# The residual stream of a decoder's FFN is added in the last chunk of hidden pairs instead of the second

## The chip, the cores and the metric

The program runs on 1 core of one Trainium2 chip. The metric is device time in microseconds (us) of one execution. The kernel before takes 2130.71 us, the median of 3 runs (2129.2 to 2131.78).

## What is computed

A trunk of two pre-norm residual layers over a stream of 1024 positions by 1024 features in float32. Layer 0 has a mixer of short convolution and mLSTM, layer 1 a spatial-gating MLP; each layer ends with a SwiGLU FFN, and a final norm follows. The change is in the FFN, which both layers call:

```python
def swiglu(xn, w_in, w_out):
    h = xn @ w_in
    g, up = h[..., :D_FF], h[..., D_FF:]
    return (jax.nn.silu(g) * up) @ w_out

x = x + swiglu(rmsnorm(x, norm_ffn[layer]), ffn_w_in[layer], ffn_w_out[layer])
```

D_FF is 2816, which is 22 slices of 128 hidden features.

## The kernel before

The stream lies transposed, features on the 128 partitions: tile `x[d][c]` holds feature rows `d` (0 to 7) and the position half `c` (0 or 1), 128 x 512 float32, 256 KB. Every product is three matmuls (`mm3`, lines 115 to 117) of a high and a low part.

**The FFN** (`swiglu`, line 390) first makes the hidden slices and stores them, as sums and differences, in DRAM (`hd` for 9 pairs of slices, `td` for the last 4 slices). It then multiplies them by `w_out` with Winograd's scheme of seven block products in place of eight (`STEPS`, line 351; step `s` runs from 0 to 6). The nine pairs are cut into four chunks, `PAIRS = (2, 2, 2, 3)`. A **unit** is one chunk `ch` and one pair of feature rows `dp` (rows 2 dp and 2 dp + 1); there are 16 of them, chunk by chunk and `dp` 0 to 3 in each. A unit of chunks 0 to 2 has 7 x 2 x 3 = 42 matmuls, one of chunk 3 has 7 x 3 x 3 = 63. Chunk 3 is followed by a **tail** (`part`, line 592), which adds the last four slices directly, column half 0 for all eight `d`, then column half 1.

For each unit, SP loads two pieces of weights (`Halves.load`, line 313: tiles `st`, 256 KB each, 384 KB in chunk 3), one unit or two ahead through four buffers; ACT and DVE cut them into high and low parts and their sums (lines 323, 324, 334 to 337). The hidden blocks of the next chunk come in during the current one by `bring` (line 524): tiles `f0h` of 256 KB, 28 for chunks 1 and 2, 42 for chunk 3, 16 for the tail, most of them in the later units of a chunk (`spread` and `ending`, lines 547 and 548). They go on SP's queue, between the weights.

**The results of a unit** go through `sink` (line 498). In chunk 0 they open the tiles `x[d][c]` (`keep`, line 486). In later chunks, steps 0, 1 and 6 add into `x[d][0]` on DVE (line 484), while for `x[d][1]` a difference is first formed in a tile `e` (lines 491 and 494) and then added into `x[d][1]` by a DMA that accumulates, which POOL issues:

```python
def gather(dst, src):
    nc.gpsimd.dma_start(dst, src, accum_op=ALU.add)
```

The stream from before the FFN, `x_in`, is in DRAM. It is added by the same kind of DMA, at the end of a unit: four tiles (two `d`, two `c`), 16 in each layer. Line 510 says in which chunk:

```python
if s == 6 and ch == 1:
    for d in rows:
        for c in range(2):
            gather(x[d][c][:, :HALF], x_in[d * P : (d + 1) * P, c * HALF : (c + 1) * HALF])
```

Everything else that reads `x` comes in the tail (line 601: `x[d][c]` plus the tail's product, on DVE), which then feeds the norm that follows and, in layer 0, a store of `x` to DRAM by POOL (line 254).

A scheduler orders the instructions of each engine beforehand; on the chip each engine's list runs in order, and a DMA waits on the engine that issues it until its semaphores allow it. In the rows below, `f0x<-x_dram` is a transfer of `x_in`, `f0x<-f0e` one of the tiles `e`, both of layer 0; `f1x` and `f1e` are layer 1's.

Of the kernel before, what the change touches and what calls it, by code (L numbers as in the profile page):

```python
# [26 lines left out]
PAIRS = (2, 2, 2, 3)  # L27
# [16 lines left out]
def trunk(ctx, tc, x_t, vecs, b_gate, b_s, ws_t, we, we_v, we_g, we_o, wo_u, wo_v, wo_o, wf_in, wf_out, out_t):  # L44
# [12 lines left out]
    def slot(name, dt=F32):  # L57
        return slots.tile([P, SLOT], dt, tag="s", name=name)
# [328 lines left out]
    def gather(dst, src):  # L387
        nc.gpsimd.dma_start(dst, src, accum_op=ALU.add)  # L388

    def swiglu(layer, normed, todo, spans, after):  # L390
# [87 lines left out]
        def onto(dp, ch):  # L478
            opening = ch == 0
            rows, hold = (2 * dp, 2 * dp + 1), {}  # L480

            def add(d, c, t):
                to = x[d][c][:, :HALF]
                nc.vector.tensor_tensor(to, t, to, op=ALU.add)

            def keep(d, c, ps):
                t = slot(f"{name}x{d}{c}" if opening else f"{name}e{d}{c}")
                if opening:
                    x[d][c] = t
                hold[d, c] = t[:, :HALF]  # L490
                nc.scalar.copy(hold[d, c], ps)

            def less(d, c, p, q):
                nc.vector.tensor_tensor(hold[d, c], p, q, op=ALU.subtract)  # L494
                if not opening:
                    gather(x[d][c][:, :HALF], hold[d, c])

            def sink(s, ps):
                d0, d1 = rows
                if s in (0, 6) and opening:  # L500
                    keep(d0 if s == 0 else d1, 0, ps)
                elif s in (0, 1, 6):
                    add(d1 if s == 6 else d0, 0, ps)
                elif s in (2, 3):
                    keep(d0 if s == 2 else d1, 1, ps)
                elif s == 4:
                    less(d1, 1, hold[d1, 1], ps)
                else:
                    less(d0, 1, ps, hold[d0, 1])
                if s == 6 and ch == 1:  # L510
                    for d in rows:
                        for c in range(2):
                            gather(x[d][c][:, :HALF], x_in[d * P : (d + 1) * P, c * HALF : (c + 1) * HALF])

            return sink
# [626 lines left out]
```

## Time and profile before

| what | value |
|---|---|
| median of the runs | 2130.71 us |
| the profiled execution | 2129.71 us, span 2128.0 us |
| TensorE (PE) busy | 2084.4 us, 98% of the span; mean granted clock 0.992 |
| DVE, ACT, POOL busy | 65%, 39%, 13% of the span |
| DMA | 327.89 MB, mean 154 GB/s; mean busy share of a slice from 0.1 to 0.9 or more |
| of that, on POOL's queue | 116.46 MB |
| chain that ended last | PE 88%, DMA 7%, issue 2%, DVE 2%, ACT 1% |
| transfers of `x_in`, each layer | 16 of 256 KB, 8.1 us (layer 0) and 7.9 us (layer 1) from issue to landing |

How to read it: PE is busy nearly all the time, so the span shortens where PE waits or where its matmuls run slowly. The stretch of the four chunks and the tail is read window by window; in layer 0 chunk 0 ends at 943 us, chunk 2 at 1041, chunk 3 at 1102, in layer 1 at 1914, 2011 and 2068. A DMA share is the mean busy share of the core's 16 DMA engines; it can pass 1 a little.

### The profile page before, as it was taken

How to read it: one execution, taken by the hardware profiler on the slowest of the kernel's cores; microseconds unless marked ns; L12 is line 12 of the kernel's file. 1: busy time of each engine (PE TensorE's matmuls, PEld its weight loads, DVE VectorE, ACT ScalarE, POOL GpSimd, SP SyncE). 2: the span in 40 equal slices, each digit the busy share in tenths (PEclk: the TensorE clock that was granted, in tenths of full speed). 3: DMA queues.
4: the chain of work that ended last, by engine and by line, in shares of the span. 5: the costliest groups of instructions: out<-in, count | busy, mean ns of one | idle time of the engine just before them, and what ended most of it. 6: DMA issues, size and time to landing. Idle time of an engine off the chain costs nothing.

```text
span 2128.0 us, 25497 instructions
## 1 busy us (share of the span) xinstructions
PE 2084.4 (98%) x9294; PEld 1685.9 (79%) x9294; DVE 1377.6 (65%) x2176; ACT 825.0 (39%) x1277; POOL 278.0 (13%) x453
## 2 busy tenths in 40 slices
PE   9999999999999999998999999999999999998998
PEld 7878888888888878875688888888888888876777
DVE  6236665568787777655556666666878777655566
ACT  5111122345444444332235743444444444432234
POOL 0000000003221121103111000002212112103110
PEclk9999999999999999999999999999999999999999
DMA  5121111536453344579974221445534334479962
GB/s 170 59 76 60 45 50 50 198 128 154 155 186 129 138 169 149 199 243 270 304 219 139 89 70 40 168 158 109 198 127 180 129 139 168 142 277 278 335 185 80
DMA packets 131934, 327.89 MB, mean 154 GB/s; under 512 B 17072, under 2 KB 19152, under 8 KB 131808
## 3 DMA queue, kind: packets, MB, share of 16 engines
q1 hardware_dynamic: 88912, 209.77, 28.7%
q0 software_dynamic: 42752, 116.46, 18.8%
q8 instruction: 73, 1.20, 0.2%
q14 instruction: 53, 0.43, 0.1%
q10 hardware_dynamic: 144, 0.03, 0.0%
HBM read 213.98 MB, written 91.24 MB: 143 GB/s over the span
## 4 chain that ended last, share of the span: by engine, by line
PE 88%; DMA 7%; issue 2%; DVE 2%; ACT 1%; POOL 0%; SPq 0%; DVEq 0%; ACTq 0%; POOLq 0%
PE Af1i L115 4%; PE Af1i L116 3%; PE Af1i L117 3%; PE Af0i L115 3%; PE Af0i L116 3%; PE Af0i L117 3%; DMA st_f1o<-wf_out 2%; DMA st_f0o<-wf_out 2%; PE Bf1i L115 2%; PE Bf1i L117 2%; PE Bf1i L116 2%; DMA f1h<-hd 2%; PE Bf0i L116 2%; PE Bf0i L115 2%; PE Bf0i L117 2%
## 5 line engine op out<-in xcount | busy, mean ns | idle before, releaser
L254 POOL DMA_DIRECT2D x_dram<-xe x16 | 8.7, 541 | 452.7 <-DVE xe L268 447.7
L254 POOL DMA_DIRECT2D x_dram<-xo x16 | 8.7, 541 | 276.7 <-DVE xo L268 271.7
L109 ACT CAST hi_eo<-st_eo 128x1024 fp32r<-128x1024 f32 x20 | 21.0, 1049 | 48.9 <-PE ep L116 30.6
L453 DVE TENSOR_TENSOR f1q<-f1q,Af1i 128x512 f32<-128x512 f32 x20 | 13.7, 687 | 36.9 <-PE Af1i L117 36.9
L453 DVE TENSOR_TENSOR f0q<-f0q,Af0i 128x512 f32<-128x512 f32 x20 | 13.7, 687 | 35.6 <-PE Af0i L117 35.6
L323 ACT CAST hix_f0i<-st_f0i 128x1024 fp32r<-128x1024 f32 x20 | 21.1, 1053 | 39.1 <-PE Af0i L116 25.0
L323 ACT CAST hix_f1i<-st_f1i 128x1024 fp32r<-128x1024 f32 x20 | 21.1, 1053 | 38.9 <-PE Af1i L116 25.1
L388 POOL DMA_DIRECT2D f0x<-f0e x24 | 22.5, 1031 | 90.8 <-DVE f0e L494 88.8
L323 ACT CAST hiy_f1i<-st_f1i 128x1024 fp32r<-128x1024 f32 x20 | 21.1, 1054 | 31.2 <-PE Bf1i L116 30.7
L388 POOL DMA_DIRECT2D f1x<-f1e x24 | 21.8, 917 | 87.2 <-DVE f1e L494 81.4
L323 ACT CAST hiy_f0i<-st_f0i 128x1024 fp32r<-128x1024 f32 x20 | 21.1, 1055 | 31.1 <-PE Bf0i L116 30.5
L443 DVE TENSOR_TENSOR f1b<-Cf1i,f1b 128x512 f32<-128x512 f32 x20 | 13.8, 688 | 26.6 <-issue 17.9
L443 DVE TENSOR_TENSOR f0b<-Cf0i,f0b 128x512 f32<-128x512 f32 x20 | 13.7, 687 | 26.6 <-issue 17.9
L116 PE MATMUL f1y<-f1h,hi_f1o 128*128 128x256 f32 (+1 forms) x96 | 30.8, 321 | 0.0
L115 PE MATMUL f1y<-f1h,hi_f1o 128*128 128x256 f32 (+1 forms) x96 | 30.8, 321 | 0.0
L117 PE MATMUL f1y<-f1h,lo_f1o 128*128 128x256 f32 (+1 forms) x96 | 30.6, 319 | 0.0
L109 ACT CAST hi_oo<-st_oo 128x1024 fp32r<-128x1024 f32 x16 | 16.8, 1052 | 35.1 <-PE op L116 26.9
L109 ACT CAST hi_evw<-st_evw 128x1024 fp32r<-128x1024 f32 x8 | 8.4, 1050 | 55.5 <-PE ek L116 36.6
L323 ACT CAST hia_f1i<-st_f1i 128x1024 fp32r<-128x1024 f32 x20 | 21.0, 1050 | 22.2 <-PE Cf1i L116 18.4
L323 ACT CAST hia_f0i<-st_f0i 128x1024 fp32r<-128x1024 f32 x20 | 21.0, 1050 | 22.1 <-PE Cf0i L116 18.4
L110 DVE TENSOR_TENSOR lo_eo<-st_eo,hi_eo 128x1024 fp32r<-128x1024 f32 x20 | 24.5, 1223 | 7.6 <-ACT hi_eo L109 7.6
L268 DVE TENSOR_TENSOR xe<-ep,xe 128x512 f32<-128x512 f32 x16 | 11.0, 690 | 27.5 <-PE ep L117 27.4
(3189 smaller groups left out, 7419.6 us busy)
## 6 DMA issues: line engine op xcount, KB each, us to landing
f0h<-hd SPq DMA_DIRECT2D x126, 256.0 KB, 6.7
f1h<-hd SPq DMA_DIRECT2D x126, 256.0 KB, 6.2
st_f0i<-wf_in SPq DMA_DIRECT2D x40, 512.0 KB, 3.5
st_f1i<-wf_in SPq DMA_DIRECT2D x40, 512.0 KB, 3.5
st_eo<-we_o SPq DMA_DIRECT2D x16, 512.0 KB, 3.6
st_oo<-wo_o SPq DMA_DIRECT2D x16, 512.0 KB, 3.5
st_f0o<-wf_out SPq DMA_DIRECT2D x24, 256.0 KB, 5.2
f0x<-f0e POOLq DMA_DIRECT2D x24, 256.0 KB, 7.1
```

Of the source, the lines that this page charges most:

```text
L109: nc.scalar.copy(hi[:, part], st[:, part])
L110: nc.vector.tensor_tensor(lo[:, part], st[:, part], hi[:, part].bitcast(F32), op=ALU.subtract)
L115: nc.tensor.matmul(ps, lhsT=lh, rhs=rh, start=first, stop=False, skip_group_check=more)
L116: nc.tensor.matmul(ps, lhsT=lh, rhs=rl, start=False, stop=False, skip_group_check=more)
L117: nc.tensor.matmul(ps, lhsT=ll, rhs=rh, start=False, stop=last, skip_group_check=more)
L254: nc.gpsimd.dma_start(x_at[0][d * P : (d + 1) * P, c * HALF : (c + 1) * HALF], x[d][c][:, :HALF])
L268: nc.vector.tensor_tensor(x, ps, x, op=ALU.add)
L323: nc.scalar.copy(hi, src)
L388: nc.gpsimd.dma_start(dst, src, accum_op=ALU.add)
L443: nc.vector.tensor_tensor(r, ps, r, op=ALU.add)
L453: nc.vector.tensor_tensor(st["q"], st["q"], ps, op=ALU.subtract)
```

## The change

One line: the 16 transfers of `x_in` of each layer are issued at the end of the units of chunk 3, the last, and no longer at those of chunk 1.

```diff
@@ -507,7 +507,7 @@
                     less(d1, 1, hold[d1, 1], ps)
                 else:
                     less(d0, 1, ps, hold[d0, 1])
-                if s == 6 and ch == 1:
+                if s == 6 and ch == len(PAIRS) - 1:
                     for d in rows:
                         for c in range(2):
                             gather(x[d][c][:, :HALF], x_in[d * P : (d + 1) * P, c * HALF : (c + 1) * HALF])
```

The lists of PE, ACT, DVE and SP keep their instructions and their order, apart from buffer numbers; only POOL's list is changed. In layer 0 (layer 1 moves alike), POOL's list from the first difference tile of chunk 1 reads as follows; `f0x` are the tiles `x[d][c]`, `f0e` the tiles `e`, `x_dram` is `x_in`. Before, chunk 1, units 0 and 1:

```order
L388 DMA f0x_6963<-x_dram_98 128x512
L388 DMA f0x_6990<-f0e_7369 128x512
L388 DMA f0x_6982<-f0e_7361 128x512
L388 DMA f0x_6990<-x_dram_98 128x512
L388 DMA f0x_7025<-x_dram_98 128x512
L388 DMA f0x_6982<-x_dram_98 128x512
L388 DMA f0x_7044<-x_dram_98 128x512
L388 DMA f0x_7079<-f0e_7462 128x512
L388 DMA f0x_7063<-f0e_7446 128x512
L388 DMA f0x_7079<-x_dram_98 128x512
```

The same place now:

```order
L388 DMA f0x_6990<-f0e_7369 128x512
L388 DMA f0x_6982<-f0e_7361 128x512
L388 DMA f0x_7079<-f0e_7458 128x512
L388 DMA f0x_7063<-f0e_7442 128x512
L388 DMA f0x_7176<-f0e_7555 128x512
```

The difference tiles of chunks 1 and 2 now follow each other with nothing between them. POOL's list at the end of chunk 3 (units 2 and 3) and the first row of the tail, before:

```order
L388 DMA f0x_7176<-f0e_8405 128x512
L388 DMA f0x_7160<-f0e_8378 128x512
L388 DMA f0x_7273<-f0e_8515 128x512
L388 DMA f0x_7257<-f0e_8504 128x512
L254 DMA x_dram_99<-f0x_6963 128x512
```

And now:

```order
L388 DMA f0x_7176<-f0e_8397 128x512
L388 DMA f0x_7160<-f0e_8370 128x512
L388 DMA f0x_7176<-x_dram_98 128x512
L388 DMA f0x_7211<-x_dram_98 128x512
L388 DMA f0x_7160<-x_dram_98 128x512
L388 DMA f0x_7230<-x_dram_98 128x512
L388 DMA f0x_7273<-f0e_8511 128x512
L388 DMA f0x_7257<-f0e_8500 128x512
L388 DMA f0x_7273<-x_dram_98 128x512
L388 DMA f0x_7324<-x_dram_98 128x512
L388 DMA f0x_7257<-x_dram_98 128x512
L254 DMA x_dram_99<-f0x_6963 128x512
```

The transfers of `x_in` stand between the difference tiles of chunk 3, and the last three of them behind the last difference tile. `f0x_7273`, `f0x_7324` and `f0x_7257` are `x[7][1]`, `x[7][0]` and `x[6][1]`.

## Rows read from the trace of the kernel before

**Rows 1.** PE timeline: last full step-6 matmul of chunks 0, 2, 3 (start us, us).

```profile
913.66 0.39 PE L117 MATMUL Af0o<-f0h,loy_f0o 128*128 128x512 f32 x1
...
942.80 0.39 PE L117 MATMUL Af0o<-f0h,loy_f0o 128*128 128x512 f32 x1
...
1040.86 0.40 PE L117 MATMUL Af0o<-f0h,loy_f0o 128*128 128x512 f32 x1
...
1101.67 0.39 PE L117 MATMUL Af0o<-f0h,loy_f0o 128*128 128x512 f32 x1
...
1884.44 0.39 PE L117 MATMUL Af1o<-f1h,loy_f1o 128*128 128x512 f32 x1
...
1913.60 0.39 PE L117 MATMUL Af1o<-f1h,loy_f1o 128*128 128x512 f32 x1
...
2010.21 0.39 PE L117 MATMUL Af1o<-f1h,loy_f1o 128*128 128x512 f32 x1
...
2068.23 0.40 PE L117 MATMUL Af1o<-f1h,loy_f1o 128*128 128x512 f32 x1
```

**Rows 2.** Windows: stretch, PE, PEld, DVE, ACT, POOL busy (x), clock, DMA share, GB/s.

```profile
904.00:943.00 39.00, 37.32 (x157) 28.60 (x156) 22.69 (x43) 15.54 (x29) 0.54 (x1) 1.00 0.70 239
943.00:1041.00 98.00, 86.46 (x348) 66.87 (x347) 56.79 (x104) 28.54 (x50) 27.14 (x31) 0.95 1.04 292
1041.00:1102.00 61.00, 57.64 (x235) 44.38 (x234) 31.52 (x46) 16.64 (x24) 7.73 (x9) 0.97 0.78 238
1102.00:1126.00 24.00, 24.00 (x106) 19.42 (x105) 16.25 (x25) 10.58 (x17) 4.39 (x8) 1.00 0.45 153
2011.00:2069.00 58.00, 56.41 (x234) 44.26 (x233) 31.33 (x46) 17.07 (x24) 7.17 (x9) 0.97 0.75 229
2069.00:2091.00 22.00, 22.00 (x97) 17.78 (x96) 10.58 (x15) 9.22 (x15) 0.00 (x0) 1.00 0.07 13
1988.00:2022.00 34.00, 33.31 (x141) 25.87 (x139) 17.63 (x29) 9.25 (x16) 5.16 (x6) 1.00 1.07 353
```

**Rows 3.** DMA issues, chunk 0, 904 to 943: queue, count, KB each, median us to landing.

```profile
st_f0o<-wf_out SPq DMA_DIRECT2D x7, 256.0 KB, 2.8
```

**Rows 4.** DMA queues and issues, chunks 1 and 2, 943 to 1041: packets, MB, share of 16 engines.

```profile
q1 hardware_dynamic: 11204, 20.66, 59.0%
q0 software_dynamic: 4320, 7.87, 44.8%
...
f0x<-x_dram POOLq DMA_DIRECT2D x16, 256.0 KB, 8.1
...
st_f0o<-wf_out SPq DMA_DIRECT2D x12, 256.0 KB, 7.9
```

**Rows 5.** Timelines of SP, DVE and PE around the largest stall of chunk 1.

```profile
959.69 3.14 SPq L317 DMA_DIRECT2D st_f0o<-wf_out  x2
...
972.22 0.43 DVE L334 TENSOR_TENSOR s_f0o<-st_f0o,st_f0o 128x256 f32<-128x256 f32 x1 [6.20 <-DMA st_f0o<-wf_out]
...
974.25 0.80 PE L115 MATMUL Bf0o<-f0h,hix_f0o 128*128 128x512 f32 x1 [4.74 <-ACT f0e L491]
```

**Rows 6.** PE timeline, the largest wait in chunk 3 of layer 0.

```profile
1055.92 0.50 PE L115 MATMUL Af0o<-f0h,hia_f0o 128*128 128x512 f32 x1 [2.09 <-ACT hia_f0o L323]
```

**Rows 7.** DMA issues, chunk 3, 1041 to 1102.

```profile
st_f0o<-wf_out SPq DMA_DIRECT2D x6, 384.0 KB, 7.4
```

**Rows 8.** Timelines of SP, POOL and DVE at the tail's start.

```profile
1093.36 0.86 SPq L108 DMA_DIRECT2D st_f0o<-wf_out  x2
...
1098.98 0.86 POOL L388 DMA_DIRECT2D f0x<-f0e  x1 [9.40 <-DVE f0e L494]
...
1124.33 0.69 DVE L601 TENSOR_TENSOR f0x<-f0y,f0x 128x512 f32<-128x512 f32 x1
```

**Rows 9.** All transfers of layer 0's difference tiles, issue to landing.

```profile
DMA to landing us min/median/max: 3.3/7.1/14.7
```

## The prediction, made before the change was run

> **What bounds the kernel now.** I read the PE timeline first, to see how long the units take. A clean unit of 42 matmuls is seen in chunk 0, which has no accumulating transfer: from one chunk end to the next marker three units take 942.80 - 913.66 = 29.14 us in layer 0 and 29.16 in layer 1 [rows 1], 9.71 us each, or 0.2313 us for a matmul. A unit of chunk 3 (63 matmuls) should then take 14.57 us. Against this the eight units of chunks 1 and 2 need 77.7 us and took 98.06 in layer 0 and 96.61 in layer 1 [rows 1]: 20.4 and 18.9 us are lost, 39.3 together. Chunk 3 (58.3 us) took 60.81 and 58.02 [rows 1], so it loses only 2.5 us and nothing.
>
> The windows say what is full in those two chunks. In chunk 0 the DMA engines are busy at 0.70; in chunks 1 and 2 at 1.04, while PE works 86.5 of 98 us at a granted clock of 0.95; in chunk 3 they are at 0.78, in the tail of layer 0 at 0.45, and in layer 1 at 0.75 and then 0.07 [rows 2]. The granted clock of 0.95 is a mean of stretches at 2.4 GHz and short ones at 1.2 GHz that follow PE's waits: the matmul after a wait of 4.74 us takes 0.80 us [rows 5], where 0.39 is usual [rows 1].
>
> The DMA view shows who is delayed: a 256 KB weight piece lands 2.8 us after its issue in chunk 0 [rows 3] and 7.9 us in chunks 1 and 2, where the 16 transfers of x_in run and take 8.1 us each [rows 4]. The timelines show how this reaches PE: two pieces issued at 959.69 are still missing when DVE wants them, DVE stands 6.20 us until 972.2, ACT's copy of a result comes late behind it, and PE waits 4.74 us at 974.25 [rows 5]. So PE is the bound, with the DMA engines in its way for two chunks of each layer.
>
> **The change part by part.** It removes nothing: 16 transfers in each layer leave chunk 1 and are issued in chunk 3. What one costs the DMA engines follows from the queues' shares: POOL's queue was busy 44.8% of 98 us = 43.9 us for 7.87 MB, thirty transfers of 0.262 MB, so 1.46 us of all 16 engines each; SP's queue took 59.0% = 57.8 us for 20.66 MB, 0.73 us for the same size [rows 4]. An accumulating transfer costs twice a plain one. The 16 are 23.4 us of DMA time for each layer.
>
> (1) Chunks 1 and 2, gain. Without the 16, the DMA work there is 57.8 + 43.9 - 23.4 = 78.3 us against 77.7 us of PE work. The engines stay nearly full, but no longer late. Whether being full hurts by itself is shown by 1988 to 2022, at the end of chunk 2 of layer 1, after the last transfer of x_in: DMA at 1.07, and yet PE idle for only 0.7 of 34 us at full clock [rows 2]. At that rate 98 us would keep 2 us of loss; the other bound is that half of today's loss, about 10 us, stays, because the blocks for chunk 3 still come in bursts. Between these I take 5 us for each layer, nearer to the row without x_in. The gain is 20.4 - 5 = 15.4 and 18.9 - 5 = 13.9, together **29.3 us** (bounds 19.3 and 35.3).
>
> (2) Chunk 3, cost. Twelve of the 16 run inside it (the last four are issued as it ends): 12 x 1.46 = 17.5 us more DMA work. Layer 0 has 0.78 x 61 = 47.6 there, so 65.1 us; at the share of 1.04 that chunks 1 and 2 reached this fits in 62.6 us, against 60.8 that the chunk takes. Layer 1 has 0.75 x 58 = 43.5, so 61.0, and 58.7 against 58.0. The excess of 1 to 2 us runs over into the tail, whose shares of 0.45 and 0.07 leave room [rows 2]. Weight pieces will land later than their 7.4 us [rows 7], but a unit here is 14.57 us long instead of 9.71. The wait of 2.09 us at 1055.92 [rows 6] comes ahead of the first transfer of x_in and stays. Bounds: nothing, and 1.23 us for each transfer, which is today's loss (39.3 / 32), so 14.8 for each layer. I take 2 us for each layer, nearer to the shares: **4 us**.
>
> (3) The queue of POOL. It issues as many transfers as before, at 0.86 us each. A transfer into x[d][1] must wait until the difference before it into the same tile has landed (7.1 us, at most 14.7 [rows 9]), and holds what is behind it, the next unit's differences. In chunk 3 POOL stood 9.40 us with nothing to do before the first difference of the last unit [rows 8], so these fit: nothing.
>
> (4) The tail. DVE's additions there now wait for x_in, where those of chunks 2 and 3 no longer do. DVE runs its list in order, so one late tile holds the whole tail. The tightest is x[7][0], which stands on POOL behind x[7][1]. In today's times: the difference of x[7][1] is issued at 1098.98 and lands 7.1 us later, x[7][1] and x[7][0] follow at 0.86 us each, and x[7][0] lands 8.1 us after that, at 1115.9; the addition is due at 1124.33 [rows 4, 8, 9]. There are 8.4 us to spare: nothing. With the longest landing of 14.7 us for both it would be at 1130.1, 5.8 us late.
>
> (5) The tail's last weights are issued at 1093.36 [rows 8], 8.5 us before it begins, and its third pair of rows needs the first of them only 11 us after its start (four tiles of 12 matmuls at 0.2313 us). If they land some us later, the tail hardly sees it: nothing.
>
> The Trainium skill says otherwise about the direction: its page DMA: Bandwidth & Descriptors, Rules for kernel authors, advises to issue a DMA early and wait for it late, and this change does the reverse. In this trace the early issue is what loses 39.3 us, because a transfer that nobody needs yet runs beside weights that are needed at once; by the rule the price would be that of the second rival below.
>
> The sum is 29.3 - 4 = 25.3 us less than the profiled execution's 2129.71, so 2104.4; the median of the runs is 1.0 us above that execution, so I say **2105.4 us**.
>
> **The rivals.**
>
> *It makes no difference.* The weights would be late without x_in too, since the 28 and 42 hidden blocks fill the engines: 78.3 of 77.7 us remain. Or chunk 3 takes over the loss at the same 1.23 us for each of 24 transfers, 29.5 us, which cancels 29.3. For it: the share near 1. Against it: the window at 1.07 that lost nearly nothing [rows 2], and the growth from 2.8 to 7.9 us when x_in is there [rows 3, 4]. Time: 2130.7.
>
> *Slower: the transfers delay chunk 3's weights more than chunk 1's.* The pieces are 384 KB there in place of 256, so each transfer could cost 1.5 x 1.23 = 1.84 us; 24 of them cost 44.2 us, against a gain of 29.3: 2130.7 + 14.9 = 2145.6. It decides once the pieces land so late that the slack of a unit is used up, which in chunks 1 and 2 happened at 7.9 us and 9.71 us a unit. For it: they land at 7.4 us already [rows 7]. Against it: 14.57 us a unit, and a share of 0.78. The rule of the Trainium skill named above would come out here.
>
> *Half is given back.* Chunk 3 loses half of 29.5 us: 2130.7 - 29.3 + 14.8 = 2116.2. This is the forecast's mechanism with a larger second term, and I count it with the forecast.
>
> That the change does something else than it says can be left out: POOL's list shows the 16 rows in their new places, and the other lists are as before.
>
> **How the numbers follow.** A measurement of this kernel can tell about 0.2%, 4.3 us, from no change. The forecast, half given back included, has a chance of 0.82, no difference 0.08, slower 0.10; these are the chances of the three signs too. The range begins at 2092, near the case that all 39.3 us go (2091.4). It ends at 2124: with the low gain of 19.3 and half of chunk 3's upper bound (14.8 of 29.6) the time would be 2126.2, and I leave out the last of that with the two rivals.
>
> **What would show it.** Right: in chunks 1 and 2 a unit takes about 10.3 us in place of 12.2, the weight pieces land in 4 to 6 us, PE's clock is at 1.00 nearly throughout, and x_in's 16 transfers appear between the end of chunk 3's first unit and some 10 us after its last. DMA in chunk 3 is at 1.0 or more. Wrong: chunks 1 and 2 still take over 90 us (first rival); chunk 3 takes over 70 us with DVE or ACT waiting for weights (second); or DVE's additions in the tail wait for a DMA and the tail grows (step 4).

## The result, and the profile after

| | median of the runs | lowest to highest |
|---|---|---|
| before, beside the change | 2131.24 us | 2129.2 to 2132.28 us, 4 runs |
| the change | 2103.27 us | 2101.49 to 2104.22 us, 4 runs |

The ratio is 0.9869 (95% interval 0.9852 to 0.9886): 28.0 us less, where 25.3 were forecast. The profiled execution of the change took 2101.49 us, its span 2099.8 us, 28.2 less than the span before.

The page of the change: busy time of each engine, then the chain that ended last.

```profile
PE 2076.8 (99%) x9294; PEld 1682.8 (80%) x9294; DVE 1376.7 (66%) x2176; ACT 824.9 (39%) x1277; POOL 277.3 (13%) x453
...
PE 95%; DMA 4%; DVE 1%; ACT 0%; issue 0%; SPq 0%; DVEq 0%; ACTq 0%
```

PE now holds 95% of the chain instead of 88%. The PE timeline gives the unit ends, by the same step-6 matmul as in [rows 1]: the first unit of chunk 0 and chunks 0, 2 and 3 of layer 0, then chunks 0, 2 and 3 of layer 1.

```profile
913.29 0.39 PE L117 MATMUL Af0o<-f0h,loy_f0o 128*128 128x512 f32 x1
...
942.41 0.39 PE L117 MATMUL Af0o<-f0h,loy_f0o 128*128 128x512 f32 x1
...
1023.84 0.40 PE L117 MATMUL Af0o<-f0h,loy_f0o 128*128 128x512 f32 x1
...
1085.14 0.39 PE L117 MATMUL Af0o<-f0h,loy_f0o 128*128 128x512 f32 x1
...
1897.04 0.39 PE L117 MATMUL Af1o<-f1h,loy_f1o 128*128 128x512 f32 x1
...
1978.21 0.39 PE L117 MATMUL Af1o<-f1h,loy_f1o 128*128 128x512 f32 x1
...
2039.55 0.40 PE L117 MATMUL Af1o<-f1h,loy_f1o 128*128 128x512 f32 x1
```

The differences of such ends, in both layers, make the ledger:

| stretch | before, us | change, us | difference |
|---|---|---|---|
| layer 0, chunks 1 and 2 | 98.06 | 81.43 | -16.63 |
| layer 0, chunk 3 | 60.81 | 61.30 | +0.49 |
| layer 1, chunks 1 and 2 | 96.61 | 81.17 | -15.44 |
| layer 1, chunk 3 | 58.02 | 61.34 | +3.32 |
| layer 1, from the end of chunk 3 to the end of the span | 59.77 | 60.25 | +0.48 |
| all the rest | | | -0.4 |

The windows of the change show the same in the engines: chunk 0, chunks 1 and 2, chunk 3 and the tail's first half of layer 0, then chunks 1 and 2 of layer 1 (columns as in [rows 2]).

```profile
904.00:943.00 39.00, 37.32 (x158) 28.61 (x157) 22.48 (x42) 15.91 (x30) 0.37 (x1) 1.00 0.69 239
943.00:1025.00 82.00, 81.72 (x351) 65.07 (x350) 57.80 (x104) 28.20 (x50) 14.16 (x17) 1.00 0.98 306
1025.00:1085.00 60.00, 56.14 (x228) 43.23 (x227) 29.20 (x43) 15.95 (x23) 17.56 (x21) 0.97 0.96 255
1085.00:1109.00 24.00, 24.00 (x105) 19.43 (x104) 15.91 (x23) 10.33 (x16) 6.77 (x11) 1.00 0.91 253
1897.00:1978.00 81.00, 80.96 (x348) 64.43 (x348) 56.71 (x103) 28.59 (x50) 13.65 (x16) 1.00 0.98 309
```

In chunks 1 and 2 PE is busy for 81.72 of 82 us at a granted clock of 1.00 (2.4 GHz), where it was busy for 86.46 of 98 at 0.95 [rows 2]. The DMA engines are still at 0.98. They are as good as full, and yet the eight units take only 3.7 us more than the 77.7 us of clean ones. Chunk 3 has gone from 0.78 to 0.96 and the tail's first 24 us from 0.45 to 0.91: the transfers now fill what stood empty there. The two halves of chunk 3 differ:

```profile
1025.00:1055.00 30.00, 26.14 (x98) 18.92 (x97) 13.81 (x23) 7.57 (x11) 6.44 (x8) 0.94 0.86 223
1055.00:1085.00 30.00, 30.00 (x131) 24.31 (x130) 15.39 (x21) 8.38 (x12) 11.12 (x14) 1.00 1.05 287
```

PE stands 3.9 us in the first half, at a DMA share of 0.86 (1.6 us in the kernel without `x_in` below), and not at all in the second, at 1.05. So the share alone does not say where PE waits.

The DMA view of the change, chunks 1 and 2 of layer 0 (compare [rows 4]):

```profile
q1 hardware_dynamic: 11574, 21.34, 72.5%
q0 software_dynamic: 2020, 3.68, 25.6%
...
st_f0o<-wf_out SPq DMA_DIRECT2D x11, 256.0 KB, 4.5
```

POOL's queue held 25.6% of 82 us, 21.0 us for 3.68 MB, or fourteen transfers of 1.50 us; SP's held 59.5 us for 21.34 MB, 0.73 us for 0.262 MB. The prices of the prediction, 1.46 and 0.73, hold. A weight piece lands after 4.5 us and no longer 7.9.

### The profile page after: what moved, and what is told of

Same layout as the page of the kernel before. It is cut to its first block, busy times and chain, and to the rows that moved or that the text cites. A ratio compares the mean times of both kernels' runs of the same rounds, so it can differ in the third digit from the quotient of the medians.

```text
span 2099.8 us, 25505 instructions
## 1 busy us (share of the span) xinstructions
PE 2076.8 (99%) x9294; PEld 1682.8 (80%) x9294; DVE 1376.7 (66%) x2176; ACT 824.9 (39%) x1277; POOL 277.3 (13%) x453
## 3 DMA queue, kind: packets, MB, share of 16 engines
q1 hardware_dynamic: 88912, 209.77, 29.3%
## 4 chain that ended last, share of the span: by engine, by line
PE 95%; DMA 4%; DVE 1%; ACT 0%; issue 0%; SPq 0%; DVEq 0%; ACTq 0%
PE Af0i L115 4%; PE Af1i L115 4%; PE Af0i L116 4%; PE Af1i L116 4%; PE Af1i L117 4%; PE Af0i L117 4%; PE Bf1i L115 2%; PE Bf1i L117 2%; PE Bf0i L116 2%; PE Bf0i L115 2%; PE Bf0i L117 2%; PE Bf1i L116 2%; PE Af1o L115 2%; PE Af1o L117 1%; PE Af1o L116 1%; PE op L115 1%
## 5 line engine op out<-in xcount | busy, mean ns | idle before, releaser
L323 ACT CAST hiy_f1i<-st_f1i 128x1024 fp32r<-128x1024 f32 x20 | 21.1, 1053 | 31.3 <-PE Bf1i L116 30.7
L443 DVE TENSOR_TENSOR f1b<-Cf1i,f1b 128x512 f32<-128x512 f32 x20 | 13.8, 688 | 26.6 <-issue 17.9
L443 DVE TENSOR_TENSOR f0b<-Cf0i,f0b 128x512 f32<-128x512 f32 x20 | 13.8, 688 | 26.6 <-issue 17.9
```

What stands on the lines that cost most here:

```text
L323: nc.scalar.copy(hi, src)
L443: nc.vector.tensor_tensor(r, ps, r, op=ALU.add)
```

## The experiments

Four theories were on trial. My own, A: a transfer of `x_in` costs DMA time, and that time is paid where the engines have none to spare and weights are wanted at once. Against it stood: B, that POOL's list (16 issues and their waits between the difference tiles) was the cost; that the additions were, whatever they move; and, C, that the time falls simply the later the transfers are issued. Each kernel below is an edit of the kernel before, where nothing else is said. The unit ends of each were read as above; "chunks 1 and 2" and "chunk 3" stand for layer 0 / layer 1.

### The transfers stay in chunk 1 but move almost nothing

```diff
-                            gather(x[d][c][:, :HALF], x_in[d * P : (d + 1) * P, c * HALF : (c + 1) * HALF])
+                            gather(x[d][c][:, :8], x_in[d * P : (d + 1) * P, c * HALF : c * HALF + 8])
```

> The 32 transfers of x_in stand in chunk 1 again, as before, with the same places on POOL's queue and the same waits, but each moves 8 of 512 columns (most of x_in is left out of the sum). Theory A (the 23.4 us of DMA time per layer that they take from the weights is what costs): about 2100 us, between 2097 and 2105, no slower than with the change. Theory B (their place on POOL's queue costs: the difference tiles wait behind them and give their buffers back late): 2125 to 2132, as before the change.

Measured: 2099.63 us, ratio 0.9855 (0.984 to 0.9869). Chunks 1 and 2 took 81.65 / 84.28, chunk 3 59.06 / 61.26, in the profiled execution, which at 2103.51 us is the longest of the four (the others took 2099.38 to 2099.68). The DMA view of its chunks 1 and 2, layer 0 (943 to 1025):

```profile
q1 hardware_dynamic: 11492, 21.19, 71.2%
q0 software_dynamic: 4320, 3.74, 30.7%
...
f0x<-x_dram POOLq DMA_DIRECT2D x16, 4.0 KB, 5.4
```

All sixteen are there, between the same difference tiles and in the same order on POOL, and with as many packets as before (4320). The time is no longer than that of the change, and 3.0 us above that of the kernel without `x_in` below. So the place in POOL's list and the packets cost 3.0 us at most, in both layers together; what the transfers move costs the rest. One thing changed along with the bytes: POOL's waits are shorter with freer DMA engines (3.15 us ahead of the second unit's transfers, where the kernel before has 8.39). But the change itself has such a wait of 9.99 us, from 1085 to 1095, and PE is busy for 24.00 of the 24 us around it. (The packets alone cost a little: 30.7% of 82 us is 25.2 us, 4.2 more than the fourteen transfers above took.)

### The transfers stay in chunk 1 but do not add

```diff
-                            gather(x[d][c][:, :HALF], x_in[d * P : (d + 1) * P, c * HALF : (c + 1) * HALF])
+                            nc.gpsimd.dma_start(x[d][c][:, :HALF], x_in[d * P : (d + 1) * P, c * HALF : (c + 1) * HALF])
```

> x_in stands in chunk 1 as before, whole, but the DMA overwrites x instead of adding to it (what chunks 0 and 1 had summed is left out of the result). Theory A: a plain transfer of the size takes 0.73 us of the DMA engines instead of 1.46, so 11.7 of 23.4 us are freed in each layer; chunks 1 and 2 have 90 us of DMA work, 86.5 us at the share of 1.04, against 98.1 measured: about 2110 us (2106 to 2116). Theory B: POOL's rows and waits are as before: 2125 to 2132.

Measured: 2113.07 us, ratio 0.9912 (0.9896 to 0.9929). Chunks 1 and 2 took 90.50 / 90.65. The DMA view of these (943 to 1034):

```profile
q1 hardware_dynamic: 11950, 22.02, 66.6%
q0 software_dynamic: 3296, 7.87, 34.5%
```

The same 7.87 MB as in [rows 4] need 34.5% of 91 us, 31.4 us, instead of 43.9: the addition is what makes such a transfer cost twice. The bytes are the same, and half of the extra DMA time is gone (some 12 us in each layer of 23.4). So is half of what `x_in` costs in chunk 1: 18.2 of 34.7 us, by the kernel without it below. What counts is DMA time, and the additions cost as far as they take it. In every pair of runs so far more DMA time taken out of chunks 1 and 2 meant less time. By the unit ends part of the gain lies outside them: of this kernel's gain 13.5 us lie in chunks 1 and 2, and 4.1 in layer 0's chunk 3 (56.76 us, where the kernel before took 60.81).

This is also what the Trainium skill says in DMA: Bandwidth & Descriptors, Issuing engines are not separate DMA queues: transfers started by different engines run on the same 16 DMA engines and interleave. The trace agrees. POOL's transfers are what delays SP's, from 4.5 to 7.9 us for a weight piece.

### Without `x_in`

```diff
-                if s == 6 and ch == 1:
+                if s == 6 and ch == len(PAIRS):
```

> x_in is never added (the residual stream is left out of the sum after each FFN). Gives the floor: what the 16 transfers still cost in chunk 3 and the tail. Theory A: the change lost 0.5 and 3.3 us in chunk 3 and 0.5 us in the last tail against before, so 2099 to 2102 us. If chunk 3 was jammed more than the units' ends show: under 2097.

Measured: 2096.59 us, ratio 0.9836 (0.9821 to 0.9851). Chunks 1 and 2 took 81.22 / 81.73, chunk 3 58.16 / 58.06. `x_in` still costs the change 6.7 us, then, of the 34.7 it cost before. That is more than expected (2099 to 2102 us for this kernel): the expectation counted from the kernel before, whose chunk 3 in layer 0 already lost 2.7 us. A weight piece in chunks 1 and 2 lands after 4.7 us here, so the 4.5 of the change is what is left without `x_in`. Nearly all of the 6.7 us is in chunk 3 (3.1 and 3.3 us), and there in the first two units of layer 0: 12.3 and 19.8 us in the change, 11.0 and 18.0 here. The windows of this kernel give the room that each stretch of layer 0 has when `x_in` is absent (chunk 0, chunks 1 and 2, chunk 3, tail):

```profile
914.00:943.00 29.00, 29.00 (x125) 22.44 (x124) 17.39 (x33) 12.33 (x23) 0.00 (x0) 1.00 0.75 247
943.00:1024.00 81.00, 80.89 (x348) 64.53 (x347) 56.85 (x103) 28.58 (x50) 12.87 (x15) 1.00 0.98 309
1024.00:1082.00 58.00, 56.39 (x233) 44.28 (x232) 31.18 (x47) 16.51 (x23) 7.21 (x9) 0.97 0.78 240
1082.00:1106.00 24.00, 24.00 (x105) 19.43 (x104) 16.77 (x24) 10.01 (x16) 4.39 (x8) 1.00 0.47 157
```

Free are 0.25 of 29 = 7.3 us, 0.02 of 81 = 1.6, 0.22 of 58 = 12.8, and 0.53 of 24 = 12.7. The sixteen need 23.4. They fit into chunk 3 and the tail (25.5) and into none of the earlier stretches.

### The other chunks

```diff
-                if s == 6 and ch == 1:
+                if s == 6 and ch == 2:
```

> x_in is added at the ends of the units of chunk 2, the third of four. Theory A: chunk 2 has the most plain traffic (42 hidden blocks for chunk 3), so the same 23.4 us per layer are lost as in chunk 1: 2124 to 2136 us. Theory C (the transfers are simply better the later they are issued): about halfway, 2112 to 2120.

Measured: 2139.97 us, ratio 1.0041 (1.0026 to 1.0056): slower than before. The waits of this kernel, layer 0, chunk 1 to the tail (943 to 1110; columns: total us, times, longest us):

```profile
ACT hia_f0o L323 <- DMA st_f0o<-wf_out: 27.9, 2, 16.1
DVE loa_f0o L324 <- ACT hia_f0o L323: 25.9, 2, 14.7
...
PE Af0o L115 <- ACT hia_f0o L323: 10.1, 2, 9.4
```

At the end of chunk 2, where the blocks for chunk 3 come in as well, chunk 3's first weight pieces are late by up to 16.1 us at ACT and PE stands 9.4 us at once: the last unit of chunk 2 took 24.4 us and the first of chunk 3 20.4. Later is not better by itself, so C falls. A had the direction right, but put the time 4 us too low at its upper end: it counted DMA time and not how late a single burst can make one piece.

```diff
-                if s == 6 and ch == 1:
+                if s == 6 and ch == 0:
```

> x_in is added at the ends of the units of chunk 0, the first. Theory A: chunk 0 has 27.3 us of DMA work in 39 us and no difference tiles, so about half of the 23.4 us per layer find room there; the rest pushes the hidden blocks of chunks 1 and 2, where nothing is free: 2108 to 2122 us, between the change and before. Theory C (the later the better): slower than before, over 2131.

Measured: 2121.4 us, ratio 0.995 (0.9935 to 0.9965), within A's bounds, and against C once more. Chunk 0's three units took 35.98 / 34.20 us instead of 29.14, and chunk 1 took 42.99 / 45.89, where it has 38.75 / 39.10 with the transfers in chunk 2.

Against the kernel without `x_in`, the sixteen transfers thus cost, for each layer, 12.4 us in chunk 0, 17.4 in chunk 1, 21.7 in chunk 2 and 3.3 in chunk 3 (half of 24.8, 34.7, 43.4 and 6.7). Chunk 0 is cheaper than 1 and chunk 3 the cheapest, as the room in the windows has it; chunk 2 is dearer than its room says, for the reason given there. Chunk 3 differs from the others in two ways, its free share and its longer units (63 matmuls in place of 42); which of the two makes it cheap, these runs do not separate.

### The change, with each transfer issued twice

```diff
-                if s == 6 and ch == 1:
+                if s == 6 and ch == len(PAIRS) - 1:
                     for d in rows:
                         for c in range(2):
                             gather(x[d][c][:, :HALF], x_in[d * P : (d + 1) * P, c * HALF : (c + 1) * HALF])
+                            gather(x[d][c][:, :HALF], x_in[d * P : (d + 1) * P, c * HALF : (c + 1) * HALF])
```

> As with the change, but each transfer of x_in is issued twice (the residual stream is added twice). Theory A: chunk 3 then has 65.1 + 17.5 = 82.6 us of DMA work, 79 us at the share of 1.04, against 61.3 measured; what the tail takes over is free, so between 2115 and 2140 us. If chunk 3's longer units tolerate late weights whatever the load: 2103 to 2108.

Measured: 2146.78 us, ratio 1.0071 (1.0056 to 1.0086), above what A allowed. Chunk 3 grew by only 5.3 us in each layer against the change; 16.5 and 15.5 us came behind it. The waits of PE in this kernel, over the whole run:

```profile
PE ss_mix L156 <- DVE tot_mix L140: 11.3, 1, 11.3
PE f1y L115 <- ACT hi_f1o L109: 6.2, 1, 6.2
```

And those of ACT, from 1090 to 1120:

```profile
ACT hi_f0o L109 <- DMA st_f0o<-wf_out: 15.5, 2, 13.8
```

The tail's own weights come 13.8 us late, and the additions start late behind them. But the last to come in layer 0 is `x_in` itself. DVE's and PE's timelines:

```profile
1129.72 0.69 DVE L602 TENSOR_TENSOR f0x<-f0y,f0x 128x512 f32<-128x512 f32 x1 [4.79 <-DMA f0x<-x_dram]
...
1132.61 1.87 PE L156 MATMUL ss_mix<-ones,tot_mix 128*128 128x1 f32 x8 [11.30 <-DVE tot_mix L140]
```

This is the addition into `x[7][0]`, the tightest one of step (4) of the prediction. It waits 4.79 us for its transfer of `x_in`, so that earlier weights alone would not have brought it forward, and PE's 11.3 us wait for the norm ends behind it. In layer 1 PE waits 6.2 us for the tail's weights themselves; later the final norm is late by 4.5 us, behind an addition that waited 3.8 us for `x_in`. The room of the change is used up, then: 46.8 us more of DMA time (2 x 23.4) cost 43.5 us over the change. One thing is mixed into this: the second copy of a tile also waits on POOL for the first (34.5 us in layer 0, 5.8 at most), so the figure says that room ends, not exactly where.

### The transfers held back until the first units of chunk 3 have passed

The first two units of chunk 3 are where the change still loses. This kernel starts from the change and gives none of the transfers to the first unit, four each to the second and third, and eight to the last, and holds each behind the last difference tile issued so far.

```diff
+LATE = (
+    (), ((0, 0), (1, 0), (2, 0), (3, 0)), ((4, 0), (5, 0), (0, 1), (1, 1)),
+    ((6, 0), (7, 0), (2, 1), (3, 1), (4, 1), (5, 1), (6, 1), (7, 1)),
+)
...
-                    gather(x[d][c][:, :HALF], hold[d, c])
+                    hold["at"] = gather(x[d][c][:, :HALF], hold[d, c])
...
-                    for d in rows:
-                        for c in range(2):
+                    for d, c in LATE[dp]:
+                        with tc.issue_after(hold["at"].ins):
```

> As with the change, but x_in's transfers are held back further: none at the end of chunk 3's first unit, four after the second, four after the third, eight after the fourth, those of column half 0 first and always behind the unit's differences on POOL's queue. Theory A: without x_in chunk 3 took 58.2 and 58.1 us, with the change 61.3 in both layers, all of it in its first two units, where the last hidden blocks still come in; held back, these 3 us per layer return and the tail has room: 2097 to 2100 us. If the 6 us are spent in the tail instead: 2102 to 2106, as the change.

The change was timed again beside it, on the same chip:

> The change once more, on the same chip and with the same runs of the kernel before as the one that holds x_in back: 2101 to 2105 us.

Measured: 2100.69 us (2100.45 to 2101.21), ratio 0.9854 (0.9839 to 0.9868), against 2103.95 us (2101.88 to 2106.04), ratio 0.9867 (0.9851 to 0.9884), for the change. The 2100.69 us are 0.7 above what A named (2097 to 2100). The aim inside chunk 3 was met: 57.95 / 57.80 us, 6.9 less than in the change. But 4.0 us went again in layer 0's tail. Windows of layer 0's tail with the transfers held back:

```profile
1082.00:1105.00 23.00, 23.00 (x101) 18.61 (x101) 12.18 (x18) 8.33 (x12) 10.74 (x14) 1.00 1.09 282
1105.00:1127.00 22.00, 19.83 (x88) 16.02 (x87) 17.34 (x33) 13.22 (x20) 4.16 (x8) 0.92 0.43 154
```

And the same two stretches of the change, timed beside it:

```profile
1085.00:1109.00 24.00, 24.00 (x105) 19.48 (x104) 15.50 (x22) 9.91 (x15) 7.61 (x11) 1.00 1.00 273
1109.00:1131.00 22.00, 22.00 (x105) 17.94 (x104) 18.64 (x35) 13.93 (x21) 3.81 (x8) 1.00 0.41 148
```

With the transfers held back, DMA passes 1.09 in the tail's first half, ACT waits up to 7.0 us for the tail's weights, and PE stands 2.2 us before the norm's first product and runs at 0.92 around it (the 22 us window). A different split, six after the second unit, two after the third, eight after the last, should by A have relieved that:

```diff
-    (), ((0, 0), (1, 0), (2, 0), (3, 0)), ((4, 0), (5, 0), (0, 1), (1, 1)),
+    (), ((0, 0), (1, 0), (2, 0), (3, 0), (0, 1), (1, 1)), ((4, 0), (5, 0)),
```

> As the version that held x_in back, which won back 7 us in chunk 3 of both layers and lost 4 us in the tail of layer 0, where the tail's last weights landed late: now six transfers are issued after chunk 3's second unit and two after the third, so that the weights asked for after the third unit find less ahead of them. Theory A: the tail of layer 0 gets its 4 us back: 2096 to 2098 us. If the tail is late because of the eight transfers at its start and the norm's input: 2100 to 2101, as held back before.

> The version that held x_in back, once more beside it: 2100 to 2102 us.

Measured: 2100.93 us, ratio 0.9856 (0.9841 to 0.9871), and for the first split again 2099.88 us, ratio 0.9854 (0.9838 to 0.9871). The second split gains nothing, as the other branch of its expectation had it, and its tail has the same wait (ACT 7.2 us). Holding back is worth some 3 us over the change where both were timed together, with no run of one among the runs of the other; the intervals of the two ratios overlap. Timed again, without the change beside it, its four runs took 2097.52 to 2104.83, a range that overlaps that of the change, so the 3 us are likely and not certain. By its medians it is the fastest of the kernels that still compute everything. What exactly delays the tail's weights in layer 0 there is open: thinning the transfers of the third unit did not do it, and the eight of the last unit were not moved.

## Why the prediction was right, point by point

**The bound, and the price of an accumulating transfer**: right. Sixteen transfers out of chunks 1 and 2 brought PE there from 86.46 of 98 us to 81.72 of 82. The price of 1.46 us was measured again at 1.50 in the change, and the plain transfer showed the factor of two as the prediction had read it from two queues.

**(1) Chunks 1 and 2.** Forecast 29.3 us, measured 16.63 + 15.44 = 32.07. The term that was off is the loss that stays, taken as 5 us for each layer: it was 81.43 - 77.7 = 3.7 and 81.17 - 77.7 = 3.5, and about as much remains without `x_in` (81.22 and 81.73 us). The window at a share of 1.07 that lost nearly nothing [rows 2] should have had more weight. A unit took 81.43 / 8 = 10.2 us, where 10.3 was named, and a weight piece 4.5 us (4 to 6).

**(2) Chunk 3.** Forecast 4 us, measured 0.49 + 3.32 = 3.81, but the agreement is partly luck. Against the kernel without `x_in` the cost is 6.4 us; in layer 0 the kernel before already lost 2.7 there (60.81 against 58.16), which went at the same time. Timed again, the change took 63.00 and 60.45 us there, so a single execution gives a layer's share only to 1 or 2 us. And one sentence of this step was wrong: that the wait of 2.09 us [rows 6] comes ahead of the first transfer and stays. POOL's timeline of the change puts the first transfer ahead of the end of chunk 2. The wait is 2.3 us in both layers of the change (1.4 and 2.1 timed again) and 1.1 without `x_in`. But `x_in` in chunk 3 is not its only cause: in the kernel before it was 2.1 in layer 0 and 1.1 in layer 1. POOL's timeline:

```profile
1022.00 0.87 POOL L388 DMA_DIRECT2D f0x<-x_dram  x1 [9.57 <-DVE f0x L484]
...
1038.41 0.87 POOL L388 DMA_DIRECT2D f0x<-x_dram  x1 [6.43 <-DMA f0x<-f0e]
...
1095.31 1.76 POOL L388 DMA_DIRECT2D f0x<-x_dram  x2 [9.99 <-DMA f0x<-f0e]
1097.96 0.86 POOL L388 DMA_DIRECT2D f0x<-x_dram  x1 [0.89 <-DMA f0x<-f0e]
```

PE's waits, the three longest of the whole run:

```profile
PE Af0o L115 <- ACT hia_f0o L323: 2.3, 1, 2.3
PE Af1o L115 <- ACT hia_f1o L323: 2.3, 1, 2.3
PE eq L115 <- ACT x001h L189: 2.1, 1, 2.1
```

The first of sixteen goes out at 1022.00, before the last matmul of chunk 2 (1023.84), because PE runs steps 0 and 1 of chunk 3's first unit ahead of that matmul, and with them `x[0][0]` has its last addition of the chunk; POOL waits for that alone (DVE, line 484). The last goes out at 1097.96, 12.8 us after the end of chunk 3, so twelve of the sixteen were issued inside it, as forecast, one ahead of it and three behind. DMA was said to reach 1.0 or more in chunk 3; it was 0.96 on the mean, 0.86 in the first half and 1.05 in the second.

**(3) POOL's queue**: right that it costs nothing, though POOL does wait longer. The waits of the change, 1025 to 1109:

```profile
POOL f0x L388 <- DMA f0x<-f0e: 29.1, 8, 10.0
...
ACT hi_f0o L109 <- DMA st_f0o<-wf_out: 5.0, 2, 2.7
```

Before `x[7][1]` POOL stood 9.99 us for the landing of the difference tile, where the prediction took the median of 7.1. PE was busy throughout that wait (24.00 of the tail's first 24 us). The transfers of 4 KB show that the place in the list costs little in chunk 1 too, 3.0 us at most, though with shorter waits.

**(4) The tail's additions**: right. DVE's timeline of the change at the addition into `x[7][0]`:

```profile
1109.13 0.68 DVE L601 TENSOR_TENSOR f0x<-f0y,f0x 128x512 f32<-128x512 f32 x1
```

There is no wait ahead of it, and none of the additions of line 601 waits for a DMA. `x[7][0]` is the second of the two issued at 1095.31, so at about 1096.2; with the median of 7.7 us from issue to landing in chunk 3 it is there at about 1104. The margin was some 5 us, not 8.4, and with each transfer doubled it was gone: there this addition waited 4.79 us.

**(5) The tail's weights**: nothing, as forecast, but it was the nearest thing to going wrong. ACT waited 5.0 us for them and PE not at all. With the transfers held back this term is the one that costs. Doubled, it costs PE 6.2 us in layer 1, while in layer 0 the wait of step (4) ends last.

**The rivals.** "It makes no difference" said that the hidden blocks would make the weights late anyway; the engines did stay at 0.98, but the weights landed after 4.5 us and hardly anything was lost. The slower one priced each of 24 transfers in chunk 3 at 1.84 us; measured is 6.4 / 24 = 0.27. Its mechanism is real all the same: issued in chunk 2, the transfers delayed chunk 3's weights by just that route (2139.97 us). With twice the load in chunk 3, though, the chunk itself grew by 5.3 us in each layer, and the rest of the 43.5 came behind it.

The Trainium skill's rule of DMA: Bandwidth & Descriptors, Rules for kernel authors (issue early, wait late), weighed there against the trace, is not borne out as a rule of order here: chunk 0, the earliest, took 2121.4 us, chunk 3, the latest, 2103.95. What decided was what else the DMA engines had to carry at that time.

## What to carry to other kernels

Before moving a transfer that nobody is waiting for, write down its DMA time, from its queue's share and bytes in the trace, beside the free share of each stretch in which it could go; move it to where it fits, earlier or later, and count what spills into the next stretch. A full stretch is not yet a late one: look at what the urgent pieces' landing times do. After the move, ask which urgent transfer stands next behind it and who reads what was moved, since that is where the room ends.

## What the runs showed of the hardware that was not expected

In chunks 1 and 2 a share of 0.98 of the DMA engines over 81 us cost 3.5 us of PE's time, 1.01 over 91 us (plain transfers) 12.8, and 1.04 over 98 us 20: between full and a little overfull lies most of the price there. But the share does not set it: in the change 1.05 over the last 30 us of chunk 3 cost PE nothing. Transfers cut to 4 KB, with as many packets, still took about 0.26 us each of all 16 engines (4.2 us for sixteen) and 5.4 us to land, so cutting their bytes frees the engines without making them quick. And a burst of late transfers at the end of chunk 2 held one weight piece back far longer than the mean share of 1.01 (60.0% and 41.3% of the two queues) would suggest: the pieces of 384 KB landed after 12.8 us, where they took 8.2 in the change, by the DMA view of that kernel from 943 to 1037:

```profile
q1 hardware_dynamic: 10808, 19.94, 60.0%
q0 software_dynamic: 3811, 6.95, 41.3%
...
st_f0o<-wf_out SPq DMA_DIRECT2D x2, 384.0 KB, 12.8
```
